# Row statistics taken by column and spread through a diagonal, a last quarter of K in groups of four, and modulation steps placed one by one

## The chip, the cores and the metric

One core of one Trainium2 chip runs the kernel. The metric is the device time of one execution in microseconds (us). An execution does one inference step for 128 context tokens and 128 latent tokens with a model width of 2048, everything in float32 in memory.

## The reference, cut to what matters

```python
def rms_norm(x, w):
    y = x * lax.rsqrt(jnp.mean(x * x, axis=-1, keepdims=True) + EPS)
    return y * w

m = silu(cvec) @ w_ada + b_ada           # six parts of 2048: sh1, sc1, g1, sh2, sc2, g2
h = rms_norm(x, norm1_w) * (1 + sc1) + sh1
p = h @ w_in                             # 2048 x 8704: q, k, v of two mixers, two gates
...                                      # attention A and B, merge, w_out, residual
x = x + g2 * (relu(h2 @ w_up) ** 2 @ w_down)
```

The change concerns the first two lines of a layer: the root mean square of each token of `x`, the shift and scale `sh1`, `sc1` (called modulation), and the first part of `h @ w_in`. Both requests go through the same weights, so the kernel holds two blocks of 128 tokens, s = 0 and s = 1.

## The kernel before, in words

A product in full precision is made of three products on TensorE. The weights are split into a high part `wH` (rounded to the float32 form that TensorE takes in one pass) and a low part `wL = raw - wH`; the activations likewise into `hH` and `hL`. Each (block of K, block of tokens) then takes `hH wH + hH wL + hL wH`.

The work is a list of weight **steps** (`wsteps`). One step is one 128x1024 tile of weights, 512 KB: two K blocks of 128 rows by 512 output columns. A step has a load on the queue of SP (L175, tile `raw`), a copy on ACT that makes `wH` (`prep_hi`, L70 by way of `copy`), a subtraction on DVE that makes `wL` (`prep`, L193), and 12 products on PE (2 K blocks x 2 token blocks x 3). `run()` writes the instructions of all engines in the order of the steps: the load of step i + 8, the `wH` and `wL` of step i + 4, then the products of step i, and then whatever `at(i, ...)` hung on that step. Engines run their own streams in that order and wait for each other through semaphores. All tiles `raw`, `wH`, `wL`, `araw`, `hH`, `hL`, `u_...` come from one pool of 48 buffers of 512 KB (`G`); a load waits until the last reader of the buffer's former tile is done.

The first 72 steps are the **first pass**. It takes the nine column blocks of `w_in` that hold q, k and v (`first_units`), and goes over K in chunks (`CHUNKS`, eight chunks of two K blocks): in each chunk all nine units get the chunk's two K blocks. The sums in PSUM (`acc`) are copied to `u_...` in the first chunk (ACT) and added to it in the later ones (DVE, L330). K goes outside so that PE can begin before all of `h` is there.

`h` is made K block by K block. For that the kernel needs:

- The token statistics. x arrives transposed (`xnT`, K on the partitions). Its squares `sq` (ACT and DVE in halves, L124 and L126) are multiplied by a matrix of ones (`ps_ss`, L128), which leaves in every one of 128 rows the same 256 sums, one for each token. `rB` takes mean plus EPS on DVE (L141) and the power -0.5 on POOL (L142, against the tile of constants `pw`). `x_scale` (L147) multiplies `xnT` by `rB` in place, one group g of four K blocks at a time.
- The modulation columns. `pair_load` brings the columns of `w_ada` for two K blocks f (8 tiles `araw`, 4 MB in all), `pair_mm` multiplies them with silu(c) (`ps_ada`, L251, 32 instructions that the profile shows as 64), `ada_evac` copies the result (`S`), `ada_cols` transposes it (`ps_sel`, L267) and sums it into `shT`, `scT` (L270 to L277).
- `make_h` (L292 on DVE, L294 on ACT) applies them in place, `split_h` makes `hH` (ACT) and `hL` (DVE, L74).

For the first pair all this stands ahead of step 0. The other seven pairs hang on the steps `nf * (c - 1) + ADA_AT`, so 3, 12, 21, 30, 39, 48 and 57, each with its four parts on that step and the three behind it.

After the first pass come the gate columns of `w_in` with the attention worked in between, the merge, `w_out`, and the feed-forward part. The change leaves their instructions as they are.

Of the kernel before, what the change touches and what calls it, by code (L numbers as in the profile page):

```python
# [10 lines left out]
F32 = mybir.dt.float32  # L11
# [6 lines left out]
P = 128  # L18
D = 2048
# [19 lines left out]
SS_AT, SS_GAP = 2, 3.2  # L39
PIECES = [[2 * i, 2 * i + 1] for i in range(8)]  # L40
G2_GAP = 6
CHUNKS = [2] * 8
ADA_AT = 3

COL = {"qA": 0, "kvA": 1024, "qB": 1536, "kB": 2560, "vB": 3584, "gA": 4608, "gB": 6656}

# [2 lines left out]
def tile_hybrid_step(ctx: ExitStack, tc: tile.TileContext, a):  # L49
# [10 lines left out]
    def G(name, dt=F32):  # L60
        return gp.tile([P, 1024], dt, name=name, tag="g")
# [4 lines left out]
    def bank(name, pool_=None):  # L66
        return (pool_ or paux).tile([P, 512], F32, name=name, tag="b")
# [25 lines left out]

    onef = cp.tile([P, P], F32, name="onef")
    dve.memset(onef, 1.0)
    pw = cp.tile([P, 256], F32, name="pw")
    pool.memset(pw, -0.5)
    cpad = cp.tile([P, KC, 32], F32, name="cpad")
    pool.memset(cpad, 0.0)
# [13 lines left out]


    warm(10)
    ps_ss = bank("ps_ss")[:, 0:256]

    def square_x(g, eng):

        sq = G("sq")  # L120
        full = xnT[g].rearrange("p k s t -> p (k s t)")
        for e, c in eng:
            if e == "A":
                act.activation(sq[:, c], full[:, c], AF.Square)  # L124
            else:
                dve.tensor_tensor(sq[:, c], full[:, c], full[:, c], op=OP.mult)  # L126
        for k in range(4):
            pe.matmul(ps_ss, onef, sq[:, 256 * k:256 * k + 256], start=g == 0 and k == 0, stop=g == 3 and k == 3)  # L128

    lo_, hi_ = slice(0, 512), slice(512, 1024)  # L130
    square_x(0, [("A", lo_), ("D", hi_)])
# [5 lines left out]
                      sg.rearrange("p (s k) -> p s k", s=2), op=OP.mult)  # L137
    for g in range(1, 4):
        square_x(g, [("A", lo_), ("D", hi_)])
    rB = cp.tile([P, 256], F32, name="rB")  # L140
    dve.tensor_scalar(rB, ps_ss, 1.0 / D, EPS, op0=OP.mult, op1=OP.add)  # L141
    pool.tensor_tensor(rB, rB, pw, op=OP.pow)  # L142

    def x_scale(g, k0=0, k1=4):

        v = xnT[g][:, k0:k1].rearrange("p k s t -> p k (s t)")
        dve.tensor_tensor(v, v, rB.unsqueeze(1).to_broadcast([P, k1 - k0, 256]), op=OP.mult)  # L147


    def wsrc(w, k0, c0):  # L150

        return w[k0 // 2, c0 // 512]
# [12 lines left out]

        loads.append((i, len(loads), fn))

    def add_step(src, mm, key, half=0, nk=2):

        st = {"half": half, "mm": mm, "key": key, "i": len(wsteps), "nk": nk}  # L170
        wsteps.append(st)

        def load():
            st["raw"] = G("raw")
            sync.dma_start(st["raw"], src)  # L175
        load_at(st["i"] - LA, load)
# [6 lines left out]
    def prep_hi(st):  # L183
        st["hi"] = G("wH", F32R)
        copy(st["hi"], st["raw"])

    def prep(st):
        nk = st["nk"]
        if "hi" not in st:
            prep_hi(st)  # L190
        raw, hi = st.pop("raw"), st.pop("hi")
        lo = G("wL", F32R)
        dve.tensor_tensor(lo, raw, hi.bitcast(F32), op=OP.subtract)  # L193
        st["hl"] = tuple(t.rearrange("p (k n) -> p k n", k=nk) for t in (hi, lo))

    prep_next = [0]

# [40 lines left out]
    def pair_load(box, nsub, fb):  # L238

        for q in range(4):  # L240
            box[fb, q] = G("araw")
            sync.dma_start(box[fb, q], a["w_pair"][nsub, fb][:, 1024 * q:1024 * q + 1024])

    def pair_mm(box, j, fb):

        if j == 0:
            box["ps"] = bank("ps_ada")
        for q in range(4):
            raw = box.pop((fb, q)).rearrange("p (k n) -> p k n", k=4)
            for k in range(4):  # L250
                pe.matmul(box["ps"][32 * k:32 * k + 32, 256 * j:256 * j + 256], cpad[:, 4 * q + k, :], raw[:, k, :],  # L251
                          start=j == 0 and q == 0, stop=j == 1 and q == 3, tile_position=(0, 32 * k))

    def ada_evac(box, n=512):
        box["S"] = sp.tile([P, 512], F32, name="S", tag="S", bufs=2)
        copy(box["S"][:, 0:n], box.pop("ps")[:, 0:n])
# [3 lines left out]
    def ada_cols(box, nsub, k0, nk):  # L260

        if nsub not in mod:
            mod[nsub] = (cp.tile([P, KC, 2], F32, name=f"shT{nsub}"), cp.tile([P, KC, 2], F32, name=f"scT{nsub}"))
        shT, scT = mod[nsub]
        ps = bank("ps_sel")
        for i in range(2 * nk):
            pe.transpose(ps[:, i * P:(i + 1) * P], box["S"][:, i * P:(i + 1) * P], ident)  # L267
        ks = slice(k0, k0 + nk)
        t = SM(4 * nk, "t")
        dve.tensor_reduce(t.rearrange("p (i m) -> p i m", m=2),  # L270
                          ps[:, 0:2 * nk * P].rearrange("p (i j m) -> p i m j", j=4, m=32)[:, :, 0:2, :],
                          axis=AX.X, op=OP.add)
        tv = t.rearrange("p (k w s) -> p w k s", w=2, s=2)
        for w, dst in ((1, scT), (0, shT)):
            b = baT[:, 3 * nsub + w, ks].unsqueeze(2).to_broadcast([P, nk, 2])
            dve.tensor_tensor(dst[:, ks, :], tv[:, w], b, op=OP.add)
        dve.scalar_tensor_tensor(scT[:, ks, :], scT[:, ks, :], 1.0,  # L277
                                 nwT[:, nsub, ks].unsqueeze(2).to_broadcast([P, nk, 2]), op0=OP.add, op1=OP.mult)
# [3 lines left out]
    def make_h(k0, nk):  # L282

        shT, scT = mod[0]
        g = k0 // 4
        if k0 % 4 == 0:
            hH[g], hL[g] = (G(f"h{x}{g}", F32R).rearrange("p (k s t) -> p k s t", k=4, s=2) for x in "HL")
        for kk in range(k0, k0 + nk):
            for s in range(2):
                v = xnT[g][:, kk % 4, s, :]  # L290
                if s:
                    dve.tensor_scalar(v, v, scT[:, kk, s:s + 1], shT[:, kk, s:s + 1], op0=OP.mult, op1=OP.add)  # L292
                else:
                    act.activation(v, v, AF.Identity, scale=scT[:, kk, s:s + 1], bias=shT[:, kk, s:s + 1])  # L294

    def split_h(k0, nk):
        g, ks = k0 // 4, slice(k0 % 4, k0 % 4 + nk)
        split(hH[g][:, ks], hL[g][:, ks], xnT[g][:, ks])
# [8 lines left out]
    nf = len(first_units)  # L307
    units = {}

    def start_step(u, k0, nk):  # L310

        def mm(st):
            acc = [bank("acc", pacc) for _ in range(2)]
            wh, wl = st["hl"]
            for k in range(nk):
                g, kg = divmod(k0 + k, 4)
                for tb in range(2):
                    sh, sl = hH[g][:, kg, tb, :], hL[g][:, kg, tb, :]
                    pe.matmul(acc[tb], sh, wh[:, k, :], start=k == 0, stop=False)  # L319
                    pe.matmul(acc[tb], sh, wl[:, k, :], start=False, stop=False)  # L320
                    pe.matmul(acc[tb], sl, wh[:, k, :], start=False, stop=k == nk - 1)  # L321
            if k0 == 0:
                units[u] = G(f"u_{u[0]}{u[1]}").rearrange("p (s n) -> p s n", s=2)
            for tb in range(2):
                if k0 == 0 and (tb == 0 or nk == 2):
                    copy(units[u][:, tb, :], acc[tb])
                elif k0 == 0:
                    dve.tensor_copy(units[u][:, tb, :], acc[tb])
                else:
                    dve.tensor_tensor(units[u][:, tb, :], units[u][:, tb, :], acc[tb], op=OP.add)  # L330
        add_step(wsrc(w_in, k0, COL[u[0]] + 512 * u[1]), mm, u, nk=nk)

    def pre_at(i, fn):
        pre.setdefault(i, []).append(fn)

    def modulate(box, k0, nk):
        ada_cols(box, 0, k0, nk)
        make_h(k0, nk)
        split_h(k0, nk)

    def chunk(c, k0, nk):

        box = {}
        if c == 0:
            for j in range(nk):
                pair_load(box, 0, k0 + j)
            fns = [lambda j=j: pair_mm(box, j, k0 + j) for j in range(nk)]
            fns += [lambda: x_scale(0, 0, nk), lambda: ada_evac(box, 2 * nk * P), lambda: prep_hi(wsteps[0]),
                    lambda: modulate(box, k0, nk), lambda: x_scale(0, nk, 4)]
            for f in fns:  # L350
                pre_at(0, f)
            for g in range(1, 4):
                at(3 * g, lambda g=g: x_scale(g))
            return
        i = nf * (c - 1) + ADA_AT
        for j in range(nk):
            load_at(i, lambda j=j: pair_load(box, 0, k0 + j))
            at(i, lambda j=j: pair_mm(box, j, k0 + j))
        at(i, lambda: ada_evac(box, 2 * nk * P))
        at(i + 1, lambda: ada_cols(box, 0, k0, nk))  # L360
        at(i + 2, lambda: make_h(k0, nk))
        at(i + 3, lambda: split_h(k0, nk))

    k0 = 0
    for c, nk in enumerate(CHUNKS):
        chunk(c, k0, nk)
        for u in first_units:
            start_step(u, k0, nk)
        k0 += nk


# [75 lines left out]
                                   channel_multiplier=1)  # L447
        K2["bias"] = bias.rearrange("p h r c -> p h (r c)")

    s0 = nf * len(CHUNKS)  # L450
    load_at(s0 - nf - 8, load_consts)
    load_at(s0 - nf - 6, load_bias)

# [587 lines left out]
```

## Time and profile before

| what | value |
|---|---|
| three runs | 1442.3, 1441.74, 1442.05 us (median 1442.05) |
| profiled execution | 1441.96 us, its span 1440.1 us |
| PE busy | 1391.7 us, 97% of the span |
| DVE, ACT, POOL busy | 980.5, 639.7, 87.8 us |
| granted TensorE clock, mean | 0.984 |
| moved by DMA | 350.94 MB, mean 244 GB/s |

PE is busy nearly all the time, so a change pays where PE is idle, or where it takes instructions off PE. The profiled execution is 1.9 us longer than its span, which counts from the first to the last instruction.

### The profile page before, as it was taken

The numbers are of one execution on the slowest core, as the hardware profiler recorded it, in microseconds if no ns is written. First come the engines' busy times: TensorE is split into PE (matmuls) and PEld (weight loads), VectorE is DVE, ScalarE is ACT, GpSimd is POOL, SyncE is SP. The second block draws the span as 40 slices with busy tenths as digits, with TensorE's granted clock in tenths as the row PEclk, the third lists the DMA queues.
The fourth block names the chain that finished last, engine by engine and source line by source line (L and its number), as shares of the span: only waits on it lengthen the run. The fifth ranks groups of instructions, "written<-read, shape, count | busy, mean of one in ns | idle before, by whom it ended". The sixth has DMA issues, their size and how long they took to land.

```text
span 1440.1 us, 18855 instructions
## 1 busy us (share of the span) xinstructions
PE 1391.7 (97%) x7084; PEld 1125.8 (78%) x7084; DVE 980.5 (68%) x1305; ACT 639.7 (44%) x845; POOL 87.8 (6%) x65
## 2 busy tenths in 40 slices
PE   4399999999999999999999999999999999999998
PEld 2277777878778877778888888888888888888887
DVE  1368887988887788866674878869866354553754
ACT  1354433546454634345474454445453454434441
POOL 6500001032000000000000000000000000000000
PEclk8599999999999999999999999999999999999999
DMA  9389889776888899886456777666766465665733
GB/s 381 132 281 334 323 292 334 227 269 244 278 281 276 326 379 348 319 299 198 167 181 203 244 241 265 220 233 239 268 191 223 146 203 190 184 212 162 216 119 117
DMA packets 98939, 350.94 MB, mean 244 GB/s; under 512 B 11616, under 2 KB 12640, under 8 KB 98848
## 3 DMA queue, kind: packets, MB, share of 16 engines
q1 hardware_dynamic: 97776, 348.31, 70.8%
q0 software_dynamic: 928, 1.34, 0.3%
q8 instruction: 56, 0.92, 0.3%
q14 instruction: 35, 0.29, 0.1%
q10 hardware_dynamic: 144, 0.08, 0.0%
HBM read 346.28 MB, written 3.41 MB: 243 GB/s over the span
## 4 chain that ended last, share of the span: by engine, by line
PE 92%; POOL 3%; DVE 2%; issue 1%; ACT 1%; DMA 0%; DVEq 0%; ACTq 0%; POOLq 0%
PE acc L227 22%; PE acc L229 22%; PE acc L228 22%; PE acc L319 5%; PE acc L320 5%; PE acc L321 5%; PE ps_ada L251 4%; POOL rB L142 3%; PE ps_T L640 1%; PE ps_S L545 1%; PE ps_g L922 1%; PE acc L723 1%; PE acc L724 1%; PE acc L722 1%; DVE wL L193 1%
## 5 line engine op out<-in xcount | busy, mean ns | idle before, releaser
L193 DVE TENSOR_TENSOR wL<-raw,wH 128x1024 fp32r<-128x1024 f32 x456 | 539.7, 1220 | 255.6 <-ACT wH L70 237.8
L70 ACT ACTIVATE wH<-raw 128x1024 fp32r<-128x1024 f32 x456 | 459.6, 1054 | 201.3 <-PE acc L229 62.9
L935 DVE SCALAR_TENSOR_TENSOR gacc<-araw,cpad,gacc 128x512 f32<-128x512 f32 x256 | 175.0, 746 | 0.0
L319 PE MATMUL acc<-wH,hH 128*128 128x512 f32 x288 | 114.8, 399 | 36.8 <-ACT hH L70 36.8
L320 PE MATMUL acc<-wL,hH 128*128 128x512 f32 x288 | 113.6, 394 | 1.7 <-DVE wL L193 1.7
L321 PE MATMUL acc<-wH,hL 128*128 128x512 f32 x288 | 113.2, 393 | 0.0
L227 PE MATMUL acc<-wH,hH 128*128 128x512 f32 x256 | 104.6, 409 | 0.0
L229 PE MATMUL acc<-wH,hL 128*128 128x512 f32 x256 | 100.1, 391 | 0.0
L228 PE MATMUL acc<-wL,hH 128*128 128x512 f32 x256 | 100.0, 391 | 0.0
L319 PEld LDWEIGHTS acc<-wH,hH 128*128 128x128 f32 x288 | 54.8, 190 | 51.2 <-ACT hH L70 37.1
L812 ACT ACTIVATE up<-acc 128x512 f32<-128x512 f32 x32 | 18.9, 590 | 153.2 <-PE acc L229 145.5
L883 DVE TENSOR_TENSOR dsum<-dsum,acc 128x512 f32<-128x512 f32 x48 | 32.4, 686 | 57.4 <-PE acc L229 57.4
L320 PEld LDWEIGHTS acc<-wL,hH 128*128 128x128 f32 x288 | 54.8, 190 | 13.1 <-DVE wL L193 2.2
L321 PEld LDWEIGHTS acc<-wH,hL 128*128 128x128 f32 x288 | 54.8, 190 | 11.6
L251 PE MATMUL ps_ada<-araw,cpad 128*32 128x256 f32 x1024 | 61.1, 382 | 2.1 <-DMA araw<-in_w_pair 1.9
L227 PEld LDWEIGHTS acc<-wH,hH 128*128 128x128 f32 x256 | 48.2, 188 | 12.7 <-issue 3.4
L70 ACT ACTIVATE S<-ps_ada 128x512 f32<-128x512 f32 x16 | 9.6, 601 | 105.6 <-PE ps_ada L251 105.6
L229 PEld LDWEIGHTS acc<-wH,hL 128*128 128x128 f32 x256 | 48.0, 188 | 10.3
L228 PEld LDWEIGHTS acc<-wL,hH 128*128 128x128 f32 x256 | 48.2, 188 | 9.9 <-issue 1.0
L251 PEld LDWEIGHTS ps_ada<-araw,cpad 128*32 128x32 f32 x1024 | 30.4, 109 | 29.6 <-issue 4.6
L227 PE MATMUL acc<-wH,h21H 128*128 128x512 f32 x120 | 47.4, 395 | 0.0
L229 PE MATMUL acc<-wH,h20L 128*128 128x512 f32 x120 | 46.8, 390 | 0.0
(472 smaller groups left out, 2841.3 us busy)
## 6 DMA issues: line engine op xcount, KB each, us to landing
raw<-in_w_in SPq DMA_DIRECT2D x136, 512.0 KB, 4.8
araw<-in_w_pair SPq DMA_DIRECT2D x128, 512.0 KB, 8.0
raw<-in_w_up SPq DMA_DIRECT2D x128, 512.0 KB, 4.3
raw<-in_w_down SPq DMA_DIRECT2D x128, 512.0 KB, 4.3
araw<-in_w_gate SPq DMA_DIRECT2D x64, 512.0 KB, 5.3
raw<-in_w_out SPq DMA_DIRECT2D x32, 512.0 KB, 4.9
raw<-in_w_br_a SPq DMA_DIRECT2D x16, 512.0 KB, 6.3
raw<-in_w_br_b SPq DMA_DIRECT2D x16, 512.0 KB, 5.2
```

The source lines that it names most:

```text
L70: act.activation(out, in_, AF.Copy)
L142: pool.tensor_tensor(rB, rB, pw, op=OP.pow)
L193: dve.tensor_tensor(lo, raw, hi.bitcast(F32), op=OP.subtract)
L227: pe.matmul(acc[tb], sh, wh[:, k, :], start=f, stop=False)
L228: pe.matmul(acc[tb], sh, wl[:, k, :], start=False, stop=False)
L229: pe.matmul(acc[tb], sl, wh[:, k, :], start=False, stop=l)
L251: pe.matmul(box["ps"][32 * k:32 * k + 32, 256 * j:256 * j + 256], cpad[:, 4 * q + k, :], raw[:, k, :], start=j == 0 and q == 0, stop=j == ...
L319: pe.matmul(acc[tb], sh, wh[:, k, :], start=k == 0, stop=False)
L320: pe.matmul(acc[tb], sh, wl[:, k, :], start=False, stop=False)
L321: pe.matmul(acc[tb], sl, wh[:, k, :], start=False, stop=k == nk - 1)
L883: dve.tensor_tensor(dsum[n][:, s, :], dsum[n][:, s, :], acc[s], op=OP.add)
L935: dve.scalar_tensor_tensor(box["acc"][:, s, :], raw[:, j, :], cpad[:, 4 * kq + 2 * half + j, s:s + 1], box["acc"][:, s, :], op0=OP.mult, o ...
```

## The change

There are three edits.

**Statistics.** The squares now are the stationary operand, and one column of ones is the moving one. The sums then lie with a token on each partition, two columns for the two token blocks. Mean, EPS and power work on 128x2. The result is brought back to 256 columns through a diagonal: `ident` times `r` on DVE (`rD`), a product of ones with it on PE (`ps_r`), a copy on ACT (`rB`).

**Groups of four.** `CHUNKS` is now `[2, 2, 2, 2, 4, 4]`. A chunk of four has two steps for each unit, whose 24 products are summed in the same banks before DVE adds them to `u_...`; the first pass keeps its 72 steps.

**Modulation by its own steps.** The seven later pairs hang on the steps 3, 12, 20, 26, 31, 40 and 48, and `x_scale` of groups 1, 2, 3 on 6, 16 and 34 (before 3, 6 and 9). `wL` of step 0 is made in two halves, one ahead of `hL` and one behind it.

```diff
-CHUNKS = [2] * 8
-ADA_AT = 3
+CHUNKS = [2, 2, 2, 2, 4, 4]
+ADA_AT = [None, 3, 12, 20, 26, 31, 40, 48]
+XS_AT = {1: 6, 2: 16, 3: 34}
...
-        for k in range(4):
-            pe.matmul(ps_ss, onef, sq[:, 256 * k:256 * k + 256], start=g == 0 and k == 0, stop=g == 3 and k == 3)
+        for i in range(8):
+            pe.matmul(ps_ss[:, i % 2:i % 2 + 1], sq[:, P * i:P * i + P], onef[:, 0:1], start=g == 0 and i == 0,
+                      stop=g == 3 and i == 7)
...
-    rB = cp.tile([P, 256], F32, name="rB")
-    dve.tensor_scalar(rB, ps_ss, 1.0 / D, EPS, op0=OP.mult, op1=OP.add)
-    pool.tensor_tensor(rB, rB, pw, op=OP.pow)
+    r = SM(2, "r")
+    dve.tensor_scalar(r, ps_ss[:, 0:2], 1.0 / D, EPS, op0=OP.mult, op1=OP.add)
+    pool.tensor_tensor(r, r, pw[:, 0:2], op=OP.pow)
+    rD, rB = cp.tile([P, 2, P], F32, name="rD"), cp.tile([P, 256], F32, name="rB")
+    ps_r = bank("ps_r")[:, 0:256]
+    for s in range(2):
+        dve.tensor_scalar(rD[:, s, :], ident, r[:, s:s + 1], None, op0=OP.mult)
+    pe.matmul(ps_r, onef, rD.rearrange("p s t -> p (s t)"), start=True, stop=True)
+    copy(rB, ps_r)
...
+    def prep_lo(st, k):
+        if k == 0:
+            st["lo"] = G("wL", F32R)
+        c = slice(512 * k, 512 * k + 512)
+        dve.tensor_tensor(st["lo"][:, c], st["raw"][:, c], st["hi"].bitcast(F32)[:, c], op=OP.subtract)
...
+        for kt in range(0, nk, 2):
+            add_step(wsrc(w_in, k0 + kt, COL[u[0]] + 512 * u[1]), lambda st, kt=kt: mm(st, kt), u)
...
+            for fn in [lambda: pair_mm(box, 0, 0), lambda: pair_mm(box, 1, 1), lambda: x_scale(0, 0, 2),
+                       lambda: ada_evac(box), lambda: prep_hi(wsteps[0]), lambda: ada_cols(box, 0, 0, 2),
+                       lambda: make_h(0, 2), lambda: prep_lo(wsteps[0], 0), lambda: split_h(0, 2),
+                       lambda: prep_lo(wsteps[0], 1), lambda: x_scale(0, 2, 4)]:
+                pre_at(0, fn)
             return
-        i = nf * (c - 1) + ADA_AT
+        i = ADA_AT[f]
```

On PE, ahead of step 0, the order before is this (`ps_ss` the sums, `ps_ada` the first pair's modulation, `ps_sel` its transposes, then the products of step 0):

```order
L128 MATMUL ps_ss<-sq,onef 128x256 x12
L251 MATMUL ps_ada<-araw,cpad 32x256 x32
L267 MATMUL ps_sel<-ident,S 128x128 x4
L319 MATMUL acc<-wH,hH_249 128x512
L320 MATMUL acc<-wL,hH_249 128x512
```

and now, at the same place on PE, it is this:

```order
L129 MATMUL ps_ss<-onef,sq 128x1 x24
L149 MATMUL ps_r<-rD,onef 128x256
L265 MATMUL ps_ada<-araw,cpad 32x256 x32
L281 MATMUL ps_sel<-ident,S 128x128 x4
L338 MATMUL acc<-wH,hH_272 128x512
L339 MATMUL acc<-wL,hH_272 128x512
```

The sums have twice as many products, each of one column, and the product that spreads `r` stands ahead of the pair's 32, which queue behind it.

On DVE, from the sums to the first steps' `wL`, before:

```order
L141 TENSOR_SCALAR rB<-ps_ss 128x256
L147 TENSOR_TENSOR xnT_74<-xnT_74,rB 128x512
L270 TENSOR_REDUCE t<-ps_sel 128x8
L276 TENSOR_TENSOR scT_238<-t,cols 128x4
L276 TENSOR_TENSOR shT_237<-t,cols 128x4
L277 SCALAR_TENSOR_TENSOR scT_238<-scT_238,cols 128x4
L292 TENSOR_SCALAR xnT_74<-xnT_74,scT_238,shT_237 128x128 x2
L74 TENSOR_TENSOR hL_250<-xnT_74,hH_249 128x512
L147 TENSOR_TENSOR xnT_74<-xnT_74,rB 128x512
L193 TENSOR_TENSOR wL<-raw,wH 128x1024 x8
```

and the same stretch of DVE now:

```order
L143 TENSOR_SCALAR r<-ps_ss 128x2
L148 TENSOR_SCALAR rD<-ident,r 128x128 x2
L155 TENSOR_TENSOR xnT_74<-xnT_74,rB 128x512
L284 TENSOR_REDUCE t<-ps_sel 128x8
L290 TENSOR_TENSOR scT_261<-t,cols 128x4
L290 TENSOR_TENSOR shT_260<-t,cols 128x4
L291 SCALAR_TENSOR_TENSOR scT_261<-scT_261,cols 128x4
L306 TENSOR_SCALAR xnT_74<-xnT_74,scT_261,shT_260 128x128 x2
L199 TENSOR_TENSOR wL<-raw,wH 128x512
L75 TENSOR_TENSOR hL_273<-xnT_74,hH_272 128x512
L199 TENSOR_TENSOR wL<-raw,wH 128x512
L155 TENSOR_TENSOR xnT_74<-xnT_74,rB 128x512
```

Two multiplications by the diagonal come in, and half of step 0's `wL` now stands ahead of `hL`.

On the queue of SP, the loads of the first pass, before (8 tiles `araw` are one pair, each `raw` one step):

```order
L242 DMA araw<-in_w_pair 128x1024 x8
L175 DMA raw<-in_w_in 128x1024 x8
L242 DMA araw<-in_w_pair 128x1024 x8
L175 DMA raw<-in_w_in 128x1024 x9
L242 DMA araw<-in_w_pair 128x1024 x8
L175 DMA raw<-in_w_in 128x1024 x9
L242 DMA araw<-in_w_pair 128x1024 x8
L175 DMA raw<-in_w_in 128x1024 x9
L242 DMA araw<-in_w_pair 128x1024 x8
L175 DMA raw<-in_w_in 128x1024 x9
```

and the same loads now:

```order
L256 DMA araw<-in_w_pair 128x1024 x8
L183 DMA raw<-in_w_in 128x1024 x7
L256 DMA araw<-in_w_pair 128x1024 x8
L183 DMA raw<-in_w_in 128x1024 x9
L256 DMA araw<-in_w_pair 128x1024 x8
L183 DMA raw<-in_w_in 128x1024 x8
L256 DMA araw<-in_w_pair 128x1024 x8
L183 DMA raw<-in_w_in 128x1024 x6
L256 DMA araw<-in_w_pair 128x1024 x8
L183 DMA raw<-in_w_in 128x1024 x5
L256 DMA araw<-in_w_pair 128x1024 x8
L183 DMA raw<-in_w_in 128x1024 x9
```

The pairs move forward past loads of steps, and there are only six and five steps between the third, fourth and fifth of the later pairs' loads. The number of transfers is the same.

More of the change, by code (lines that the diff above doesn't have):

```diff
@@ L95, in tile_hybrid_step @@
     dve.memset(onef, 1.0)
-    pw = cp.tile([P, 256], F32, name="pw")
+    pw = cp.tile([P, 64], F32, name="pw")
     pool.memset(pw, -0.5)
@@ L115, in tile_hybrid_step @@
     warm(10)
-    ps_ss = bank("ps_ss")[:, 0:256]
+    ps_ss = bank("ps_ss")
     def square_x(g, eng):
@@ L166, in load_at, with add_step @@
         loads.append((i, len(loads), fn))
-    def add_step(src, mm, key, half=0, nk=2):
-        st = {"half": half, "mm": mm, "key": key, "i": len(wsteps), "nk": nk}
+    def add_step(src, mm, key, half=0):
+        st = {"half": half, "mm": mm, "key": key, "i": len(wsteps)}
         wsteps.append(st)
@@ L185, in prep_hi @@
         copy(st["hi"], st["raw"])
+    def prep_lo(st, k):
[3 more added lines that the diff above has]
+        dve.tensor_tensor(st["lo"][:, c], st["raw"][:, c], st["hi"].bitcast(F32)[:, c], op=OP.subtract)
     def prep(st):
-        nk = st["nk"]
         if "hi" not in st:
             prep_hi(st)
[L191 to L194, printed above, removed]
+        if "lo" not in st:
+            st["lo"] = G("wL", F32R)
+            dve.tensor_tensor(st["lo"], st["raw"], st["hi"].bitcast(F32), op=OP.subtract)
+        st.pop("raw")
+        st["hl"] = tuple(st.pop(n).rearrange("p (k n) -> p k n", k=2) for n in ("hi", "lo"))
     prep_next = [0]
@@ L308, in tile_hybrid_step, with start_steps, mm @@
     units = {}
-    def start_step(u, k0, nk):
-        def mm(st):
-            acc = [bank("acc", pacc) for _ in range(2)]
+    def start_steps(u, k0, nk):
+        box = {}
+        def mm(st, kt):
+            if kt == 0:
+                box["acc"] = [bank("acc", pacc) for _ in range(2)]
+            acc = box["acc"]
             wh, wl = st["hl"]
-            for k in range(nk):
-                g, kg = divmod(k0 + k, 4)
+            last = kt + 2 == nk
+            for k in range(2):
+                g, kg = divmod(k0 + kt + k, 4)
                 for tb in range(2):
                     sh, sl = hH[g][:, kg, tb, :], hL[g][:, kg, tb, :]
-                    pe.matmul(acc[tb], sh, wh[:, k, :], start=k == 0, stop=False)
+                    pe.matmul(acc[tb], sh, wh[:, k, :], start=kt == 0 and k == 0, stop=False)
                     pe.matmul(acc[tb], sh, wl[:, k, :], start=False, stop=False)
-                    pe.matmul(acc[tb], sl, wh[:, k, :], start=False, stop=k == nk - 1)
+                    pe.matmul(acc[tb], sl, wh[:, k, :], start=False, stop=last and k == 1)
+            if not last:
+                return
             if k0 == 0:
@@ L324, in mm @@
             for tb in range(2):
-                if k0 == 0 and (tb == 0 or nk == 2):
+                if k0 == 0:
                     copy(units[u][:, tb, :], acc[tb])
-                elif k0 == 0:
-                    dve.tensor_copy(units[u][:, tb, :], acc[tb])
                 else:
                     dve.tensor_tensor(units[u][:, tb, :], units[u][:, tb, :], acc[tb], op=OP.add)
-        add_step(wsrc(w_in, k0, COL[u[0]] + 512 * u[1]), mm, u, nk=nk)
+            box.clear()
+        for kt in range(0, nk, 2):
+            add_step(wsrc(w_in, k0 + kt, COL[u[0]] + 512 * u[1]), lambda st, kt=kt: mm(st, kt), u)
@@ L333, in pre_at, with mod_pair @@
     def pre_at(i, fn):
         pre.setdefault(i, []).append(fn)
[L336 to L353, printed above, removed]
+    def mod_pair(f):
+        box, k0 = {}, 2 * f
+        if f == 0:
+            for j in range(2):
+                pair_load(box, 0, j)
+            for fn in [lambda: pair_mm(box, 0, 0), lambda: pair_mm(box, 1, 1), lambda: x_scale(0, 0, 2),
[3 more added lines that the diff above has]
+                pre_at(0, fn)
@@ L354, in chunk @@
             return
-        i = nf * (c - 1) + ADA_AT
-        for j in range(nk):
+        i = ADA_AT[f]
+        for j in range(2):
             load_at(i, lambda j=j: pair_load(box, 0, k0 + j))
             at(i, lambda j=j: pair_mm(box, j, k0 + j))
[L359 to L362, printed above, removed]
+        at(i, lambda: ada_evac(box))
+        at(i + 1, lambda: ada_cols(box, 0, k0, 2))
@@ L364, in tile_hybrid_step @@
+        at(i + 2, lambda: make_h(k0, 2))
+        at(i + 3, lambda: split_h(k0, 2))
+    for f in range(8):
+        mod_pair(f)
+    for g, i in XS_AT.items():
+        at(i, lambda g=g: x_scale(g))
     k0 = 0
-    for c, nk in enumerate(CHUNKS):
-        chunk(c, k0, nk)
+    for nk in CHUNKS:
         for u in first_units:
-            start_step(u, k0, nk)
+            start_steps(u, k0, nk)
         k0 += nk
@@ L448, in load_bias @@
         K2["bias"] = bias.rearrange("p h r c -> p h (r c)")
-    s0 = nf * len(CHUNKS)
+    s0 = len([st for st in wsteps if st["key"] in first_units])
     load_at(s0 - nf - 8, load_consts)
```

## The prediction

> **What bounds the kernel now.** I read the page's head and then the span by stretches, to find where PE, busy 97% of the span, has its idle time.
>
> ```profile
> span 1440.1 us, 18855 instructions
> ...
> PE 1391.7 (97%) x7084; PEld 1125.8 (78%) x7084; DVE 980.5 (68%) x1305; ACT 639.7 (44%) x845; POOL 87.8 (6%) x65
> ```
>
> ```profile
> 0.00:20.00 20.00, 16.04 (x108) 9.07 (x108) 4.10 (x9) 4.51 (x8) 7.88 (x9) 1.00 0.91 358
> 20.00:57.80 37.80, 0.63 (x4) 0.42 (x4) 1.77 (x8) 2.78 (x6) 34.89 (x1) 0.52 0.68 271
> 64.00:291.00 227.00, 227.00 (x1342) 178.98 (x1341) 179.83 (x262) 97.68 (x123) 9.21 (x13) 1.00 0.83 293
> ```
>
> The columns of the stretches are the length, then busy time of PE, PE's weight loads, DVE, ACT and POOL, then granted clock, DMA share and GB/s. PE idles 37.2 us between 20 and 57.8 us, three quarters of the 48.4 us that it idles in the whole span (1440.1 - 1391.7). In the first pass proper, 64 to 291 us, it idles not at all. In the gap POOL alone works. The chain of waits, then the timeline (start, length, instruction, wait before it), say at what:
>
> ```profile
> 13.61 41.29 POOL rB L142
> 54.92 0.69 DVE xnT L147
> 57.12 0.64 ACT hH L70
> 60.27 0.80 PE acc L320
> ```
>
> ```profile
> 18.91 0.64 PE L251 MATMUL ps_ada<-araw,cpad 128*32 128x256 f32 x8 [0.64 <-DMA araw<-in_w_pair]
> 19.62 0.60 ACT L70 ACTIVATE S<-ps_ada 128x512 f32<-128x512 f32 x1 [10.34 <-PE ps_ada L251]
> 20.36 0.63 PE L267 MATMUL ps_sel<-ident,S 128*128 128x128 f32 x4 [0.81 <-ACT S L70]
> 55.53 0.18 DVE L270 TENSOR_REDUCE t<-ps_sel 128x8 f32<-128x32 f32 x1
> 55.95 0.16 DVE L277 SCALAR_TENSOR_TENSOR scT<-scT,cols 128x4 f32<-128x4 f32 x1
> 56.15 0.60 DVE L292 TENSOR_SCALAR xnT<-xnT,scT,shT 128x128 f32<-128x128 f32 x2
> 57.78 0.69 DVE L74 TENSOR_TENSOR hL<-xnT,hH 128x512 fp32r<-128x512 f32 x1 [1.03 <-ACT hH L70]
> 57.80 0.79 PE L319 MATMUL acc<-wH,hH 128*128 128x512 f32 x1 [36.82 <-ACT hH L70]
> 60.27 0.80 PE L320 MATMUL acc<-wL,hH 128*128 128x512 f32 x1 [1.67 <-DVE wL L193]
> ```
>
> One POOL instruction, the power on 128x256, runs from 13.6 to 54.9 us. The modulation columns are ready for DVE at 20.99 (20.36 + 0.63), but DVE works in order, and its `x_scale` waits for `rB` ahead of them. The second product of step 0 (L320, 60.27) then waits for `wL` as well. From there PE never idles again in this pass, so the whole rest of the kernel moves by as much as that product moves, provided the loads keep up.
>
> **The power.** What a narrow power costs stands in the groups of POOL (count | busy, mean ns):
>
> ```profile
> L142 POOL TENSOR_TENSOR rB<-rB,pw 128x256 f32<-128x256 f32 x1 | 41.3, 41277 | 11.5 <-DVE rB L141 11.5
> L109 POOL TENSOR_TENSOR rq<-rs,pw 128x4 f32<-128x4 f32 x1 | 1.0, 1049 | 0.1
> L109 POOL TENSOR_TENSOR r<-rs,pw 128x1 f32<-128x1 f32 x2 | 1.2, 580 | 0.2
> ```
>
> It goes by columns. 128x2 lies between 0.58 and 1.05 us; by a straight line I take 0.74.
>
> **The sums.** The program has 16 products `ps_ss` before, the trace 32: each is two passes of PE. Now there are 32 products, so 64 passes with a full 128x128 weight load and one column each. No row shows that shape. These are nearest (the rows of the sums from the timeline, the others from the chain):
>
> ```profile
> 4.78 0.69 DVE L126 TENSOR_TENSOR sq<-xnT 128x512 f32<-128x512 f32 x1 [3.19 <-DMA xnT<-in_xT]
> 5.46 1.99 PE L128 MATMUL ps_ss<-sq,onef 128*128 128x256 f32 x8 [0.26 <-ACT sq L124]
> 7.72 5.34 PE L128 MATMUL ps_ss<-sq,onef 128*128 128x256 f32 x24
> 8.65 0.69 DVE L126 TENSOR_TENSOR sq<-xnT 128x512 f32<-128x512 f32 x1 [0.59 <-DMA xnT<-in_xT]
> ```
>
> ```profile
> 73.90 3.59 PE ps_ada L251 x64
> 80.44 0.44 PE ps_sel L267 x4
> 328.23 1.79 PE ps_S L545 x16
> ```
>
> The sixteen `ps_S` passes have a full weight load and 128 columns: 0.112 us each (1.79/16). The `ps_ada` passes load a quarter of the weights: 0.056 (3.59/64), the low end. The high end is 0.22, what a pass of the old sums took (5.34/24). I take 0.112, the row with the same weight load. Four groups of 16 passes then take 1.79 us each; from 5.46, with 0.43 for the two warming products after the first group, they end at 13.05, where the old ones ended (13.06). The last squares, ready at 9.34, are no limit.
>
> **The rest of the statistics.** From 13.05: mean and EPS on 128x2 0.16 (the L277 row), power 0.74, two diagonals at 0.30 (half of the L292 row), the spreading product's two passes 0.45, the copy at most 0.60 (the S row is twice as wide), `x_scale` 0.69. With 0.05 for each hand-over that is 16.5. DVE reads the modulation columns at 21.0, so this has 4.5 us of cover. The nearer limit is PE's queue: the pair's 64 passes now stand behind the spreading product, which starts about 14.7. They take 3.59 us once their data is there, so they end near 18.8 if nothing else held them; but the last tile arrives at 18.91 and its eight passes end at 19.55, as before. That is 0.8 us of slack. If the sums end later than about 13.9, every microsecond costs one.
>
> **Where step 0 then starts.** Before, 2.27 us went from the reduction (55.53) to the first product (57.80). Starting the reduction at 21.02, the first product comes at 23.29. The half of `wL` is ready at 21.02 + 0.62 (columns, 56.15 - 55.53) + 0.60 + 0.69 = 22.93, so the second product follows at the half clock's spacing of 0.43 (the first chain row below), at 23.72. `hL`, from 23.27 to 23.96, is there for the third at 24.15. The move is 60.27 - 23.72 = **36.55 us**.
>
> ```profile
> 61.06 0.43 PE acc L321
> 69.82 0.23 PE acc L319
> ```
>
> ```profile
> 21.70:66.00 44.30, 6.52 (x15) 4.76 (x16) 8.73 (x14) 6.52 (x10) 33.19 (x1) 0.50 0.59 229
> ```
>
> **The clock.** Before, it is halved from 21.7 to 66.0 us; products are 0.43 instead of 0.23 us apart until 66, so from 60.27 some 13.5 products lose 0.2 us each, 2.7 us in all. Now PE still idles from 19.55 to 23.3 but for four transposes, and I expect the same fall at 21.7 and a slow start of the same length: nothing gained or lost. The ends are 2.7 us gained, if it does not fall, and some 6 us lost, if the thin sums let it fall early (first rival).
> The Trainium skill (TensorE: Matmul & The Clock Gate, "Why this matters for your kernels") asks only for no gap over about 3 us between bursts. The gap from the transposes to step 0 would be 2.3 us (20.99 to 23.29), so by that rule the clock would stay up, which is the third rival's time. The trace speaks against it: the clock fell 0.7 us after the transposes. The same page (Part 4) says that transposes do not count as busy, and then the gap is 3.7 us and page and trace agree.
>
> **The loads.** Their number stays: 4 for x, 64 for the pairs, 72 for steps and 8 that step 71 has sent ahead, 148 tiles. Two things change: PE begins 36 us earlier, and the pairs' loads are bunched.
>
> ```profile
> 28.00:32.00 4.00, 0.00 (x0) 0.00 (x0) 0.00 (x0) 0.00 (x0) 4.00 (x1) 0.50 1.03 410
> 48.00:52.00 4.00, 0.00 (x0) 0.00 (x0) 0.00 (x0) 0.00 (x0) 4.00 (x1) 0.50 0.00 0
> ```
>
> ```profile
> araw<-in_w_pair SPq DMA_DIRECT2D x128, 512.0 KB, 8.0
> ```
>
> Unhindered they run at 410 GB/s, one tile in 1.28 us, until the pool is full at about 45 us. The first x tile is there at 4.78, so the n-th tile comes at 4.78 + 1.28(n - 1). The second pair is the 20th to 27th: its last tile comes at 38.1. Step 3 ends near 37 (13 products at 0.43, 35 at 0.23 from 23.3), and the pair's passes last to 40.6, so it arrives in time. Step 7's tile is the 28th, 39.4, and is needed near 49. The tightest stretch is steps 21 to 31: 11 steps and two pairs are 27 tiles, 34.6 us of DMA, against 11 x 2.77 (12 x 0.23) + 2 x 4.03 (3.59 and 0.44 of transposes) = 38.5 us of PE. By the order, the last buffers of the fifth later pair come free with step 25, some 20 us ahead of its use after step 31, against 8.0 us from issue to landing. So I cost the new places at nothing; the cover is this lead, and without it the price is the second rival's.
>
> **Groups of four.** DVE drops 36 additions of 0.686 us, 24.7 us:
>
> ```profile
> L330 DVE TENSOR_TENSOR u_qA<-u_qA,acc 128x512 f32<-128x512 f32 x28 | 18.9, 686 | 2.4 <-PE acc L321 2.4
> ```
>
> ```profile
> PE acc L320 <- DVE wL L193: 1.7, 1, 1.7
> ```
>
> The second row, from the list of waits, is the only wait of PE from 60 to 300 us, the one at 60.27. DVE is not what PE waits for in the pass, so these 24.7 us buy nothing. PE's products are the same 864. DVE's two diagonals and one more half `wL`, and ACT's copy, lie in the cover counted above.
>
> **The sum.** The profiled execution took 1441.96 us, 0.09 under the median of the three runs. 1441.96 - 36.55 = 1405.41; with the 0.09, **1405.5 us**.
>
> **The rivals.**
> *First: the sums run long.* If the one-column passes cost 0.15 to 0.22 us, or the clock falls during them since PE works in thin slices, they end at 15.5 to 20 us instead of 13.05. At 0.22: 5.46 + 64 x 0.22 + 0.43 = 20.0, 6.1 us beyond the 13.9 that is free. Time 1407 to 1411.6. For it: nothing shows the shape. Against it: a wider pass with the same weights took 0.112. Chance 0.20.
> *Second: the loads fall behind* in the early steps or in the bunch. If the tiles of steps 21 to 31 took 1.5 us, the 27 would need 40.5 us, 2 more than PE; with the lead in the early steps gone as well, 3 to 8 us. Time 1408.5 to 1413.5. Against it: 293 GB/s over the pass without a PE wait, 410 when free. Chance 0.08.
> *Third: the clock stays up* through the short gap: 1405.5 - 2.7 = 1402.8. Chance 0.12.
> *Fourth, slower than before:* DMA as the bound of the whole pass. The pool's fill in the long gap is a head start that goes. The 148 tiles (77.6 MB) must land before the pass can end; it ended near 291. If they took until then from 4 us on, 270 GB/s, the whole gain would be gone, and below that the kernel is slower: at 250 GB/s it ends at 314, time 1465. The windows show more at every place where PE asked for it. Chance 0.02.
> *Fifth: the narrow power costs what the wide one does,* and the kernel stays at 1442. The 0.58 us row speaks against it. Chance 0.01.
>
> **How the numbers follow.** My forecast has 0.57, with its own range of 1404 to 1407. The range 1402.5 to 1411 takes in the third rival and most of the first, and leaves out about 0.12. Within 0.2% (2.9 us, about what a measurement of this kernel can tell from no change) is the fifth alone, 0.01; slower is the fourth, 0.02; faster 0.97.
>
> **What the changed profile would show.** The power on POOL near 0.74 us at about 13.3; the first pair's last passes (`ps_ada`) still ending near 19.6; the first product of step 0 at 23.3 with no wait for `wL` behind it; half clock for 5 to 6 us from there; PE busy without a gap through the first pass, which ends near 255; 36 fewer additions on DVE with no effect. It would be wrong if the sums end after 14 us, or if PE shows waits for `araw` or `raw` between 37 and 140 us.

## The result, and the profile after

The changed kernel takes 1408.91 us (median of four runs, 1408.62 to 1410.5) against 1441.96 us for the kernel before: a ratio of 0.9773, 95% interval 0.9756 to 0.979. That is faster, as forecast, inside the range of 1402.5 to 1411, and 3.4 us slower than the 1405.5 of the likeliest case. The profiled execution took 1408.84 us with a span of 1407.1 us.

The head of the page of the changed kernel, and its clock in tenths by slices, answer to the head of before:

```profile
span 1407.1 us, 18890 instructions
...
PE 1395.7 (99%) x7118; PEld 1131.3 (80%) x7118; DVE 958.5 (68%) x1272; ACT 640.6 (46%) x846; POOL 48.7 (3%) x65
...
PEclk7999999999999999999999999999999999999999
```

PE now idles 11.4 us of its span instead of 48.4. The timeline of the start (start, length, engine, line, instruction, wait ahead of it) shows the 41 us power gone, and something else grown:

```profile
5.61 1.95 PE L129 MATMUL ps_ss<-onef,sq 128*128 128x1 f32 x16 [0.16 <-ACT sq L125]
7.85 9.59 PE L129 MATMUL ps_ss<-onef,sq 128*128 128x1 f32 x48
17.47 0.16 DVE L143 TENSOR_SCALAR r<-ps_ss 128x2 f32<-128x2 f32 x1 [7.99 <-PE ps_ss L129]
17.71 0.72 POOL L144 TENSOR_TENSOR r<-r,pw 128x2 f32<-128x2 f32 x1 [15.86 <-DVE r L143]
18.47 0.48 DVE L148 TENSOR_SCALAR rD<-ident,r 128x128 f32<-128x128 f32 x2 [0.84 <-POOL r L144]
19.01 1.22 PE L149 MATMUL ps_r<-rD,onef 128*128 128x256 f32 x2 [1.58 <-DVE rD L148]
20.16 4.64 PE L265 MATMUL ps_ada<-araw,cpad 128*32 128x256 f32 x64
25.62 0.63 PE L281 MATMUL ps_sel<-ident,S 128*128 128x128 f32 x4 [0.82 <-ACT S L71]
28.56 0.50 PE L338 MATMUL acc<-wH,hH 128*128 128x512 f32 x1 [2.31 <-ACT hH L71]
28.89 0.51 PE L339 MATMUL acc<-wL,hH 128*128 128x512 f32 x1
```

The sums of squares end at 17.44 us instead of the forecast 13.05. The first 16 one-column passes took 0.12 us each (1.95/16), the other 48 took 0.20 (9.59/48). The first pair's passes stand behind the spreading product and end at 24.8 instead of 19.55, and step 0 starts at 28.56 instead of 23.29. The windows of the same execution, cut where the records of the granted clock change (length, busy time of PE, weight loads, DVE, ACT, POOL, then clock, DMA share, GB/s), say why:

```profile
5.13:8.55 3.42, 3.26 (x28) 2.79 (x26) 2.09 (x4) 1.81 (x4) 0.00 (x0) 1.00 1.02 419
8.55:22.20 13.65, 12.07 (x65) 10.29 (x68) 2.03 (x5) 1.01 (x2) 0.72 (x1) 0.50 1.03 410
22.20:29.03 6.83, 3.70 (x54) 1.92 (x46) 2.25 (x8) 3.57 (x6) 0.00 (x0) 1.00 1.03 409
29.03:32.44 3.41, 3.41 (x10) 2.48 (x9) 3.41 (x5) 3.27 (x4) 0.00 (x0) 0.50 1.03 410
```

The clock is halved at 8.55, after 3.42 us of which PE shows itself busy for 3.26, and stays so for 13.65 us: through two thirds of the sums' passes, the spreading product and part of the pair's passes. The window of the sums alone (length, busy time of PE, weight loads, DVE, then clock, DMA share, GB/s) counts 43 of the 64 passes at half clock, 0.207 us each (8.88/43):

```profile
8.55:17.44 8.89, 8.88 (x43) 8.80 (x42) 0.00 (x0) 0.50 1.03 412
```

Three landmarks of PE follow (the first products of step 0 and step 4, and the first transposes `ps_qT` of the attention, from the timelines; the forecast for the last two is before less 36.55):

| start on PE, us | before | forecast | after |
|---|---|---|---|
| first product of step 0 | 57.80 | 23.29 | 28.56 |
| first product of step 4 | 77.42 | 40.87 | 44.98 |
| first `ps_qT` | 294.24 | 257.69 | 261.80 |
| time of the profiled execution | 1441.96 | 1405.41 | 1408.84 |

From step 4 to `ps_qT` both kernels take 216.82 us. The whole miss of 4.1 us is in the start; 0.7 us come back between `ps_qT` and the end of the execution.

### The profile page after: what moved, and what is told of

Same layout as the page of the kernel before. It is cut to its first block, busy times and chain, and to the rows that moved or that the text cites. A ratio compares the mean times of both kernels' runs of the same rounds, so it can differ in the third digit from the quotient of the medians.

```text
span 1407.1 us, 18890 instructions
## 1 busy us (share of the span) xinstructions
PE 1395.7 (99%) x7118; PEld 1131.3 (80%) x7118; DVE 958.5 (68%) x1272; ACT 640.6 (46%) x846; POOL 48.7 (3%) x65
## 3 DMA queue, kind: packets, MB, share of 16 engines
HBM read 346.28 MB, written 3.41 MB: 249 GB/s over the span
## 4 chain that ended last, share of the span: by engine, by line
PE 98%; issue 1%; ACT 0%; DVE 0%; POOL 0%; POOLq 0%; ACTq 0%
PE acc L241 24%; PE acc L243 24%; PE acc L242 24%; PE acc L338 5%; PE acc L340 5%; PE acc L339 5%; PE ps_ada L265 4%; PE ps_T L658 1%; PE ps_S L563 1%; PE ps_g L940 1%; PE acc L742 1%; PE acc L741 1%; PE acc L740 1%; PE ps_sel L281 1%; PE acc L758 0%
## 5 line engine op out<-in xcount | busy, mean ns | idle before, releaser
L243 PEld LDWEIGHTS acc<-wH,hL 128*128 128x128 f32 x256 | 48.0, 188 | 10.4
```

The costliest lines, as they stand in the source:

```text
L243: pe.matmul(acc[tb], sl, wh[:, k, :], start=False, stop=l)
```

## The experiments

Theory A: the one-column passes do not count as work for the clock, it falls to half, and the sums, the spreading product and the pair run at half speed on the path to step 0. Everything else in the change is worth little. The rivals are named with each run. Times are medians; the kernel before took 1441.5, 1441.72 and 1441.88 us beside the three sets.

**stats_only: the statistics without the rest.** The kernel before with the statistics hunks of the diff alone.

> The kernel before with the new token statistics alone: eight chunks of two, the old places of the modulation, wL of step 0 in one piece behind hL. Theory A (all of the gain is the statistics; groups of four and new places buy nothing): the changed kernel's time plus about 1.7 us, since the second product of step 0 waits for the whole wL again, so 1409.5 to 1411.5. Rival (groups of four or the new places give a part of the gain, because DVE drops 25 us of additions): 1414 or more.

Measured: 1414.61 us (1412.18 to 1416.88), ratio 0.9814 (0.98 to 0.9827). A miss for the theory's figure, and by its number the rival's. Its runs lie at two levels, 1412.2 and 1412.6, 1416.7 and 1416.9; even the lower is above the expected range, by 0.7 us at the least. The profiled one is of the upper. Its timeline shows passes at half speed from the first on, and its list of waits (us in total, times, longest) the second product's wait for the undivided `wL`:

```profile
5.43 3.47 PE L128 MATMUL ps_ss<-onef,sq 128*128 128x1 f32 x16
9.56 10.24 PE L128 MATMUL ps_ss<-onef,sq 128*128 128x1 f32 x48
```

```profile
PE acc L327 <- DVE wL L200: 2.0, 1, 2.0
```

The first 16 passes took 0.217 us each and the other 48 took 0.213, where the changed kernel's profile has 0.12 at full clock. So the clock had not risen even ahead of the sums; this is read from the passes, since the trace's first record of the clock, a rise to full, is at 27.05 us, and the page counts the time ahead of it as full. From step 4 to `ps_qT` this kernel, too, takes 216.82 us (51.91 to 268.73). So the rival's reason, that DVE's additions or the places hold the first pass up, is not in the trace; sums128_twos below settles it with a steadier start.

**rest_only: the rest without the statistics.** The changed kernel with the old sums and the power on 128x256.

> The changed kernel with the old statistics (wide power of 41 us): groups of four, new places of the modulation, wL of step 0 in halves. Theory A: the kernel before less some 2 us for the second product of step 0, which no longer waits for wL: 1439 to 1442. Rival (groups of four pay by themselves): 1430 or less. A loss here (over 1443) would mean that the bunched pairs cost something.

Measured: 1438.6 us (1438.28 to 1439.7), ratio 0.9982 (0.9973 to 0.9991); 2.9 us less than before, 0.4 under the expected range. Its list of waits has the wait for the power and none for `wL`:

```profile
PE acc L331 <- ACT hH L71: 36.8, 1, 36.8
```

The profiled execution is one of the slower ones, 1439.65 us. In it step 4 starts 1.6 us earlier than before (75.86), which is the half `wL`, and 0.6 us more is gained behind the first pass. The 24.7 us of additions that DVE drops change nothing: 216.82 us again from step 4 to `ps_qT`.

**sums128: the same passes with 128 columns moving.**

```diff
-            pe.matmul(ps_ss[:, i % 2:i % 2 + 1], sq[:, P * i:P * i + P], onef[:, 0:1], start=g == 0 and i == 0,
-                      stop=g == 3 and i == 7)
+            pe.matmul(ps_ss[:, 128 * (i % 2):128 * (i % 2) + 128], sq[:, P * i:P * i + P], onef[:, 0:128],
+                      start=g == 0 and i == 0, stop=g == 3 and i == 7)
-    dve.tensor_scalar(r, ps_ss[:, 0:2], 1.0 / D, EPS, op0=OP.mult, op1=OP.add)
+    dve.tensor_scalar(r, ps_ss[:, 0:256:128], 1.0 / D, EPS, op0=OP.mult, op1=OP.add)
```

> The changed kernel, the moving operand of the sums 128 columns of ones instead of one (the same 64 passes and weight loads; one column of the 128 equal ones is read). Theory A (the thin passes let the clock fall to half, and half clock makes a pass 0.2 us): the clock stays full through the sums, a pass takes 0.11 us, the sums end near 13.1 instead of 17.4, the first pair's passes near 19.6 instead of 24.9, the first product of step 0 comes near 23.3; time 1404 to 1406. Rival B (a pass with a full float32 weight load and nothing to hide it takes 0.2 us at any clock): sums end at 17.4 or later, time 1408.5 or more.

Measured: 1404.21 us (1404.13 to 1404.55), ratio 0.9742 (0.9729 to 0.9756), 4.7 us less than the changed kernel, for 128 times the columns. Its timeline and its windows cut by clock:

```profile
7.81 5.52 PE L129 MATMUL ps_ss<-onef,sq 128*128 128x128 f32 x48
14.90 0.70 PE L149 MATMUL ps_r<-rD,onef 128*128 128x256 f32 x2 [1.57 <-DVE rD L148]
18.93 0.64 PE L265 MATMUL ps_ada<-araw,cpad 128*32 128x256 f32 x8 [0.16 <-DMA araw<-in_w_pair]
23.84 0.50 PE L338 MATMUL acc<-wH,hH 128*128 128x512 f32 x1 [2.83 <-ACT hH L71]
```

```profile
4.02:24.50 20.48, 14.51 (x142) 10.58 (x140) 6.85 (x18) 6.80 (x12) 0.72 (x1) 1.00 1.03 412
24.50:27.90 3.40, 3.40 (x9) 2.66 (x9) 3.40 (x6) 3.08 (x4) 0.00 (x0) 0.50 1.02 408
```

A pass takes 0.115 us (5.52/48), the sums end at 13.3, the pair waits for its last tile only, and step 0 starts at 23.84. Theory A holds; rival B (0.2 us at any clock) is out. This is the start that the prediction described.

**sums32: 32 columns moving.** As sums128 with 32 for 128.

> As sums128, but with 32 columns of ones moving in each of the 64 passes. Theory A in the form 'what counts is how long the columns stream' (32 columns are a quarter of the work of 128 in the same pass): the clock falls as with one column, sums end near 17.4, time 1408 to 1410. Rival ('any moving block beyond a single column counts as work'): the clock stays, time 1404 to 1405.

Measured: 1408.76 us (1405.23 to 1409.03), ratio 0.9764 (0.9746 to 0.9781). Three of four runs are at 1408.6 to 1409.0 and one at 1405.23. In the profile the clock falls at 9.16, and the sums run to 16.8:

```profile
7.79 9.03 PE L129 MATMUL ps_ss<-onef,sq 128*128 128x32 f32 x48
```

So a quarter of the columns is not enough to hold the clock as a rule. The low run was not profiled; its mean granted clock, 0.995 against 0.993 in the other three, agrees with less time at half clock.

**late_spread: the spreading product behind the pair.**

```diff
-    pe.matmul(ps_r, onef, rD.rearrange("p s t -> p (s t)"), start=True, stop=True)
-    copy(rB, ps_r)
+    def spread_r():
+        pe.matmul(ps_r, onef, rD.rearrange("p s t -> p (s t)"), start=True, stop=True)
+        copy(rB, ps_r)
...
-            for fn in [lambda: pair_mm(box, 0, 0), lambda: pair_mm(box, 1, 1), lambda: x_scale(0, 0, 2),
+            for fn in [lambda: pair_mm(box, 0, 0), lambda: pair_mm(box, 1, 1), spread_r, lambda: x_scale(0, 0, 2),
```

> The changed kernel with the spreading product (ps_r) behind the first pair's passes on PE instead of ahead of them. Theory A (the pair's passes had their data and stood 2.8 us behind it, from 17.4 to 20.2): sums still end at 17.4 at half clock, the pair's passes run from there to about 22, the copies follow, and the first product of step 0 comes near 26.8 instead of 28.6; time 1406.5 to 1408. Rival (the pair's order is not what sets the end, since the statistics come last anyway): no change, 1408.5 to 1409.5.

Measured: 1407.19 us (1406.35 to 1408.07), ratio 0.9763 (0.9749 to 0.9776): 1.7 us less than the changed kernel, and inside the range that theory A expects. The timeline of an execution of 1407.84 us shows the pair directly behind the sums, and the spreading product behind both:

```profile
7.78 10.24 PE L129 MATMUL ps_ss<-onef,sq 128*128 128x1 f32 x48
17.95 5.19 PE L267 MATMUL ps_ada<-araw,cpad 128*32 128x256 f32 x64
23.06 0.70 PE L151 MATMUL ps_r<-rD,onef 128*128 128x256 f32 x2
```

The sums are still slow: in this execution the clock fell at 7.44, so all 48 passes of the second row took 0.213 us, the sums ended at 18.0 instead of the expected 17.4, and step 0 started at 27.71 instead of 26.8. The queue behind the spreading product was a part of the loss, not its cause.

The same execution answers a rival that no run names, that the moment at which the clock rises decides whether it falls. Here it rose at 4.03, in sums128 at 4.02. The windows from there to the fall, and the same stretch of sums128 (columns as for the changed kernel):

```profile
4.03:7.44 3.41, 2.94 (x22) 2.14 (x21) 1.76 (x4) 1.54 (x4) 0.00 (x0) 1.00 1.03 421
4.02:7.43 3.41, 2.82 (x21) 2.13 (x20) 1.64 (x4) 1.43 (x4) 0.00 (x0) 1.00 1.03 419
```

PE shows itself busy for 2.94 us with one column a pass and the clock falls, and for 2.82 us with 128 and it holds.

**sums128_twos: the old first pass on a start that holds the clock.** sums128 with `CHUNKS = [2] * 8`, the pairs on 3, 12, 21, 30, 39, 48, 57 and `XS_AT = {1: 3, 2: 6, 3: 9}`.

> sums128 with the first pass as it was before (eight groups of two, pairs on steps 3, 12, 21, 30, 39, 48, 57, x_scale on 3, 6, 9); it keeps step 0's wL in halves. Theory (groups and places are worth nothing but a few tenths): 1404 to 1405.2, that is sums128 plus 0 to 1. Rival (they are what keeps PE fed now that it starts early; the kernel with the statistics alone took 1414.6): 1406 or more, with PE waits in the first pass.

Measured: 1404.82 us (1404.77 to 1405.18), ratio 0.9745 (0.9729 to 0.976). The groups of four with the new places are worth 0.6 us (1404.82 - 1404.21; the two were run in different sets). By the timelines it lies in the attention, between the first `ps_qT` and the first transposes of the merge (260.52 us here, 259.91 in sums128); in the first pass there is nothing. Every profile with groups of four has 259.9 us there, sums128_bunch with quite other places too, and those with groups of two have 260.5 to 260.6, so it goes with the groups and not with the places; why is not shown.

**sums128_bunch: how far the pairs can be bunched.** sums128 with the pairs on 3, 6, 9, 12, 15, 18, 21 and `XS_AT = {1: 4, 2: 10, 3: 16}`.

> sums128 with the seven later pairs bunched much tighter, on steps 3, 6, 9, 12, 15, 18, 21. Where does the loads' lead end? Per pair 11 tiles at 1.28 us are 14.1 us of DMA against 3 x 2.77 + 4.03 = 12.3 us of PE, so DMA becomes the bound from step 6 to 21: 1.8 us lost for each of the last six pairs, 8 to 13 us in all less what the lead covers; time 1410 to 1417, with PE waits for araw. Rival (buffers, not bandwidth, hold the loads up, or nothing does): over 1420, or 1404 to 1406.

Measured: 1414.57 us (1414.51 to 1414.61), ratio 0.9812 (0.9796 to 0.9827), 10.4 us more than sums128, all of it ahead of `ps_qT` (267.62 against 257.20). Its windows show DMA at 408 GB/s, the rate of a load that nothing holds up (410 in the prediction), and PE no longer full; the list of waits names the pairs' tiles, for 3.7 of the 10.4 us (the rest is not taken apart):

```profile
80.00:100.00 20.00, 18.35 (x145) 11.75 (x138) 10.66 (x19) 8.04 (x12) 0.00 (x0) 1.00 1.03 408
```

```profile
PE ps_ada L265 <- DMA araw<-in_w_pair: 3.7, 7, 0.6
```

The loss lies in the expected range of 8 to 13 us, so the arithmetic of tiles against PE time is right about a distance of three steps. By the same arithmetic four steps are the edge (12 tiles, 15.4 us, against 15.1 us of PE); that was not tried.

**sums128_fill: ten warming products in the gap ahead of step 0.**

```diff
-                       lambda: ada_evac(box), lambda: prep_hi(wsteps[0]), lambda: ada_cols(box, 0, 0, 2),
-                       lambda: make_h(0, 2), lambda: prep_lo(wsteps[0], 0), lambda: split_h(0, 2),
+                       lambda: ada_evac(box), lambda: prep_hi(wsteps[0]), lambda: ada_cols(box, 0, 0, 2),
+                       lambda: warm(10), lambda: make_h(0, 2), lambda: prep_lo(wsteps[0], 0), lambda: split_h(0, 2),
```

> sums128 with ten warming products (bfloat16, 128x512, results unused) on PE between the first pair's transposes and step 0, where PE idles 2.8 us. Theory A: the clock no longer falls at 24.5 and the first eight to nine products of step 0 take 0.23 instead of 0.43: 1.6 us less than sums128, so 1402.2 to 1403.2. Rival (the fall comes from the time before, between the pair's passes and the transposes, or the fill delays step 0): no change or slower, 1404 or more.

Measured: 1404.09 us (1404.04 to 1404.2), ratio 0.9739 (0.9724 to 0.9755). The clock did hold from 6.2 us to the end, and step 3 began 1.5 us earlier than in sums128 (32.43 against 33.97), but the time is the same, 0.9 us above the expected range. The timeline shows the saving turned into a wait for the second pair's last tile, and ACT waiting for step 7's:

```profile
35.24 3.38 PE L265 MATMUL ps_ada<-araw,cpad 128*32 128x256 f32 x56
39.25 0.64 PE L265 MATMUL ps_ada<-araw,cpad 128*32 128x256 f32 x8 [0.63 <-DMA araw<-in_w_pair]
40.49 1.06 ACT L71 ACTIVATE wH<-raw 128x1024 fp32r<-128x1024 f32 x1 [7.27 <-DMA raw<-in_w_in]
```

On ACT the copies of step 3's sums (41.46) and of the pair's result (42.41) stand behind that `wH`. Of the 1.5 us, 0.6 are left at step 4 (39.82 against 40.37) and 0.1 at step 5 (43.47 against 43.58).

**fill_pair4 and sums128_pair4: the second pair one step later.** `ADA_AT = [None, 4, 12, 20, 26, 31, 40, 48]`, with and without the fill.

> sums128_fill with the second pair's passes one step later (after step 4 instead of step 3; its eight loads then stand one step tile later on the queue). Theory C (what the fill saved, 1.5 us up to step 3, went into the wait for the second pair's last tile, landed at 39.2, and for step 7's tile, landed at 40.5, behind which ACT holds its copies; the loads run at 410 GB/s and bound this place): PE has step 4's 2.8 us to do meanwhile, and the 1.4 to 1.8 us come out: 1402.2 to 1402.8. Rival (the saving went elsewhere): 1403.8 or more.

> sums128 (no fill, slow first products) with the second pair one step later. Theory C: without the fill PE reaches the second pair at 36.8, its passes took 3.6 us without a wait of note, so there is next to nothing to win: 1403.8 to 1404.4. Rival (the place alone is worth something, whatever the fill does): 1402.2 to 1403.

Measured: 1402.82 us (1402.73 to 1402.95), ratio 0.973 (0.9717 to 0.9743), with the fill; 1404.34 us (1404.11 to 1405.35), ratio 0.9741 (0.9728 to 0.9755), without. Only both together bring the 1.4 us out: the pair's passes run from 38.09 without a wait, and the first `ps_qT` comes at 255.78 instead of 257.11 with the fill alone. fill_pair4 is the fastest of all, 6.1 us under the changed kernel and 39.1 under the one before.

## Why the prediction was right or wrong, point by point

- **The power** was right: 0.72 us measured against 0.74, and the 36.8 us wait of PE is gone.
- **The sums** are the step that failed. "I take 0.112, the row with the same weight load" holds at full clock: 0.122 for the first 16 passes, 0.115 with 128 columns. But the clock fell under them and 48 passes took 0.20. That is the first rival, in the form "the clock falls during them since PE works in thin slices", which I gave 0.20. I had taken the price of the wide pass, but not its claim on the clock. The 43 passes at half clock took 8.88 us where 0.112 each gives 4.82, so they make 4.1 of the 4.4 us by which the sums ended late. They ended at 17.44, 3.5 us past the point of about 13.9 from which "every microsecond costs one", and past the 14 us that the prediction named as its sign of being wrong. The time lies in the stated range because the range took in this rival; the path of the likeliest case (1404 to 1407) was wrong here. With the spreading product (1.22 instead of 0.45) and the pair's passes (4.64 instead of 3.59) also partly at half clock, step 0 came 5.27 us late.
- **The rest of the statistics** was a little dear: two diagonals took 0.48 (0.60 taken), the copy 0.38 (0.60 as its bound).
- **The queue behind the spreading product** was seen rightly as the nearest limit; late_spread took 1.7 us off it.
- **The clock ahead of step 0.** I expected a slow start of the same length as before. It fell at 29.03 and was back at 32.44, so some 8 products were slow instead of 13.5, which gave about 1.1 us back. So the third rival did not come about; only the ten products of the fill kept the clock up. The 3.41 us at whose end it fell, 25.62 to 29.03, hold 1.10 us of PE (0.63 of transposes, 0.47 of step 0). In the kernel before, the fall at 21.7 came 2.15 us after the pair's last pass (19.55), so no gap of 3 us had passed there, whether transposes count or not, and the agreement that the prediction found is not borne out. The Trainium skill (TensorE: Matmul & The Clock Gate, "What's actually happening") describes a free-running window of about 3.4 us; the records agree, with changes at 5.13, 8.55, 22.20, 29.03 and 32.44, distances of 3.42, 13.65, 6.83 and 3.41, each 3.41 us or a multiple of it. The Trainium skill's rule against gaps (same title, "Why this matters for your kernels") did not tell of this case, since the fall at 8.55 came with PE busy 3.26 of 3.42 us.
- **The loads** kept up, as worked out: in the changed kernel PE has no wait for `raw` or `araw` in the first pass, with DMA at 371 GB/s from 75 to 130 us instead of 309. The second rival was real but a few steps away: sums128_bunch has it, and sums128_fill shows that with a faster start the second pair's last tile does bound step 4.

```profile
75.00:130.00 55.00, 55.00 (x344) 42.99 (x343) 45.19 (x72) 22.84 (x30) 0.00 (x0) 1.00 0.97 371
```

- **Groups of four** were costed at nothing in the first pass, and that is what every profile shows; behind it the groups gave 0.6 us that I had not seen (sums128_twos).
- **The sum.** 4.1 us late at step 4, less 0.7 behind the first pass, are the 3.4 us between 1405.4 and 1408.8. The sums, the spreading product and the pair cost 5.3 us; that only 3.4 were left is luck, since neither the shorter slow start nor the 0.7 us was foreseen.

## What to carry to other kernels

When a wide instruction on a slow engine is replaced by thin ones on a fast engine, price the thin ones twice: by the nearest row, and at half clock. If a stage of PE loads weights but streams few columns, widen the moving operand up to what the weight load hides; here it was free and saved 4.7 us. After a stall has gone, look for the next thing that arrives just in time (here one 512 KB tile at 39 us), because a further gain ahead of it is worth nothing until that is moved.

## What the runs showed of the hardware that was not expected

The granted clock does not follow the busy time that the profile shows: from 8.55 to 17.44 PE was busy 8.88 of 8.89 us, with full weight loads and one column each, and ran at half clock. With 32 columns it fell as well (at 9.16 in the profiled run, and by their times in two more of four), with 128 it held to the end of the sums. At half clock a one-column pass takes 0.213 us (10.24/48 in late_spread) instead of 0.12, and the weight loads slow down with it. The loads of the sums in the changed kernel (shortest, median and longest, in ns) take 186 at the shortest and 333 at the median; those ahead of 8.5 us, at full clock, have a median of 192:

```profile
L129 PEld LDWEIGHTS ps_ss<-onef,sq x64: 186/333/333, 5.6 to 17.0; 128*128 128x128 f32 x64
```

The start of the clock's window differs from execution to execution: from a trace's first record of the clock on, the changes come at multiples of 3.41 us, but that first record is at 5.13 us in the changed kernel, 4.02 in sums128 and 7.09 in sums128_twos. With one-column sums equal runs of one kernel lay up to 4.7 us apart (stats_only), with 128 columns 0.4 us (sums128) to 1.2 us (sums128_pair4). That the start of the window makes this spread is likely and not shown run by run: one execution of each kernel has a trace. The one of sums128_pair4 is of its slower kind (1405.34) and has 6.83 us of half clock at step 0, where sums128 has 3.41.
